# Two head groups of a dilated-attention trunk in Strassen block form

## The chip, the cores and the metric

The kernel runs on one core of one Trainium2 chip. The metric is the time of one execution on the device, in microseconds (us). The core has five instruction queues that run side by side and are tied together by semaphores: TensorE (PE, matrix products; PEld is its weight load), VectorE (DVE), ScalarE (ACT), GpSimd (POOL) and SyncE (SP). SP only issues transfers here; POOL issues the transfers that add to their destination, and computes a little.

## The reference

A decoder trunk of two layers on a sequence of 512 tokens with 1024 channels, all float32. Layer 1 mixes tokens by attention: three groups of eight heads, each with its own window and dilation. Layer 2 mixes by causal pooling. A SwiGLU feed-forward block follows each. The part that the change touches is the attention:

```python
qkv = (h @ w_qkv).reshape(B, S, 3, 3, 8, 128)     # h: rmsnorm(x), 512 x 1024
for g, (window, dil) in enumerate(((128, 1), (512, 4), (2048, 16))):
    o, lse = dilated_window_attention(q_g, k_g, v_g, window, dil, slopes[g])
o = sum_g softmax_g(lse) * o_g
x = x + o.reshape(B, S, 1024) @ w_out
```

For each of the 8 heads there are thus 3 groups, and for each group one product for q, one for k and one for v, each 512 x 1024 by 1024 x 128.

## The kernel before

**Precision.** Each float32 operand is split into a high part and a low part (the rest). A product is three matmuls on each 128-wide slice of the contraction: high times high, high times low, low times high. A weight tile of 128 x 1024 is loaded into a buffer `raw`; `split` makes its high part on ScalarE (L92) and its low part on VectorE (L93, raw minus high). In the "lean" form the low part is made otherwise: ScalarE writes the high part (L146) and its negative (L147), and POOL issues a transfer that adds the weight from memory onto that (L149).

**Plain and block form.** A plain product (`Product`, lines L329, L330, L332) of a group's q or k is 8 slices x 3 = 24 matmuls with 512 columns. The block form (`seven`, whose matmuls are L461 to L463 in `mult`) computes q and k of one group together as a 2 x 2 block matrix product by a Strassen scheme: 7 products of half-size blocks instead of 8, each 4 slices x 3 = 12 matmuls of 256 columns, 84 in all. Its weights (`Pair`) come as corners: two tiles of 128 x 1024 and a half tile by SP (L170 to L172), and one adding transfer by POOL (L173). They are split as "b", "s", "m" and "l"; "m" needs two additions on VectorE first (L189, L190). The other operand is the normalized input in block sums, `T`, made by `prepare(k)` for k = 0 to 3: L578, L582, L583, L587 and eight splits. Copies and additions (L489, L502, L510, L515, L516) put the seven products together.

**Order of head 0 and head 1.** Head 0 is plain in all groups. Head 1's three groups (`NSOLO = 3`) are plain too; from then on each group is in block form. The values of head 0 and 1 are plain, later ones in block form (`values12`, L632 to L634). Between products stand the attention steps: `scores0` (L716 to L725), `scores12` (L736 to L750), `merge` (L769 to L786, which scales the probabilities of both kinds: L783 on VectorE, L786 on ScalarE), `turn0` and `turn12` (transposes L799 and L820 on TensorE, copies L803, L805, L821, and L806, L825 on VectorE), and `output` (L837, L838, L844). They are hung into `seven` and `values12` as hooks by `between`.

**What sets the order.** The program's code gives an order of calls, and a scheduler of the framework lays the instructions of each engine out in a fixed sequence. Weights are pulled in by `pump`: a load when a buffer of `raw` (4) is free, a split when a buffer of `w` (5) or `half` (2) is free.

**The last head.** With head 7 the input x is loaded a second time (`xN`, L983, eight transfers of 128 x 512 by POOL) into the buffers that part of `T` occupied, for the residual sum. The output projection's weights are three plain tiles, two block pairs (`w_outp`), one plain tile. `summed` (L1022 to L1024) makes the block sums for it.

Of the kernel before, what the change touches and what calls it, by code (L numbers as in the profile page):

```python
# [15 lines left out]
P = 128  # L16
S = 512
# [22 lines left out]
NPLAIN = 4  # L40
WARM = 5
NOUT = 3
NSOLO = 3
PARTS = ((0, 2, False), (2, 10, True), (10, 18, True), (18, 22, False))
ENDS = 5
BACK = {"blocks": 3, "sums": 7}
# [19 lines left out]
def trunk(ctx: ExitStack, tc: tile.TileContext, xT, xN, norms, w_first, w_qk, w_qkp, w_v0, w_v0p, w_v12, w_out, w_outp, w_pair, w_down, w_dblock, w_pin, w_pgrp,  # L66
# [173 lines left out]
    for h in range(HEADS):  # L240
        if h == 0:
            plain(*[w_qk[u] for u in range(len(QK) - NF)])
        for g in range(3):
            if h == 1 and g < NSOLO:
                plain(*[w_qk[len(QK) - NF + 2 * g + c] for c in range(2)])
            elif h:
                pairs(w_qkp[3 * h - 3 - NSOLO + g])
        if h == 0:
            plain(w_v0[0], w_v0[1])
        elif h % 2 == 0:  # L250
            pairs(w_v0p[h // 2 - 1])
        else:
            pairs(w_v12[h // 2, 0], w_v12[h // 2, 1], shift=APART)
    plain(*[w_out[m] for m in range(NOUT)])
    pairs(w_outp[0])
    pairs(w_outp[1])
    plain(w_out[NOUT])

    def ffn_plan(layer):
# [340 lines left out]
    with tc.tile_pool(name="opool", bufs=1) as opool:  # L600
        early = [opool.tile([P, 2, S], F32R, tag=f"o{k}", name="early") for k in range(K2)]
        with tc.tile_pool(name="apool", bufs=1) as apool:
# [158 lines left out]
            def merge(h):  # L761
# [22 lines left out]
                for r in range(NT):  # L784
                    v = s12[:, r]
                    nc.scalar.activation(v, v, AF.Copy, scale=co[:, 1, r:r + 1])  # L786

            T0 = []

            def turn0(h):  # L790

                s0 = A[h]["s0"]
                if not T0:
                    T0.append(apool.tile([P, 2 * NT - 1, P], F32, name="t0"))
                    nc.vector.memset(T0[0], 0.0)
                own, before = T0[0][:, :NT], T0[0][:, NT:]
                p = ps()
                for b in range(NT):
                    nc.tensor.transpose(blk(p, b), s0[:, b, :P], ident)  # L799
                pb = p.rearrange("p (b q) -> p b q", b=NT)  # L800
                for j in range(NT):
                    c = slice(j * NI, (j + 1) * NI)
                    nc.scalar.copy(before[c, :, :c.stop], pb[c, 1:, :c.stop])  # L803
                    if j < NT - 1:
                        nc.scalar.copy(own[c, :, c.stop:], pb[c, :, c.stop:])  # L805
                    nc.vector.transpose(own[c, :, c], s0[c, :, P:])  # L806
                A[h]["t0"] = own, before
# [3 lines left out]
            def turn12(h):  # L811

                s12 = A[h]["s12"]
                if not T12:
                    T12.append(apool.tile([P, 2, NT, P], F32, name="t12"))
                    nc.vector.memset(T12[0][:, 1], 0.0)
                t12 = T12[0]
                p = ps()
                for r in range(NT):
                    nc.tensor.transpose(blk(p, r), s12[:, r, :P], ident)  # L820
                nc.scalar.copy(t12[:, 0].rearrange("p r k -> p (r k)"), p)  # L821

                for j in range(NT):
                    c = slice(j * NI, (j + 1) * NI)
                    nc.vector.transpose(t12[c, 1, :, c], s12[c, :, P:])  # L825
                A[h]["t12"] = t12
# [28 lines left out]
                 + [(late12[:, 0], late12[:, 1]), tuple(late)])  # L855
            H, T, o = {}, {}, []

            def prepare(k):

                h, t = normed(0, k, rows["row"], Held("raw"), Held("raw"))  # L860
                for i in range(2):
                    held["h", k + i * K2], b = slot("h")
                    H[k + i * K2] = b[:, 0], b[:, 1]
                    split(*H[k + i * K2], h.t[:, i * S:(i + 1) * S])
                T["11", k] = halves_of(*H[k])[0]
                T["21", k], T["22", k] = halves_of(*H[k + K2])
                for i, names in enumerate((("1", "2"), ("3", "4"))):
                    if k < 2:
                        held["t", k, i], b = slot("t")
                        b = b[:, 0], b[:, 1]  # L870
                    else:
                        c = k - 2 + 2 * i
                        b = x_tile(c, "tx", F32R), x_tile(c + K2, "tx", F32R)
                    split(*b, t.t[:, i * S:(i + 1) * S])
                    for name, v in zip(names, halves_of(*b)):
                        T[name, k] = v
                h.done()
                t.done()

            OP2 = {}  # L880
# [75 lines left out]
            for c in range(2):  # L956
# [1 line left out]
                if c == 0:  # L958
                    scores0(0)
                scaled_by(VT[c], p, True)  # L960
                prepare(2 + c)
            scores12(0)
            turn_values(0)
            scatter(0)
            for h in range(1, HEADS):
                for g in range(3):
                    if h == 1 and g < NSOLO:
# [9 lines left out]
                if h == 1:  # L977
                    O = [opool.tile([P, 2, S], F32, tag=f"o{k}", name="o") for k in range(K2)]
                    o.extend(O[h % K2][:, h // K2] for h in range(HEADS))
                if h == HEADS - 1:  # L980
                    X[:] = [x_tile(k) for k in range(KC)]
                    for k in range(KC):
                        nc.gpsimd.dma_start(X[k], xN[:, k, :])  # L983
                if h % 2 == 0:
                    VT[:] = [apool.tile([P, S], F32, tag=tag, name="vt") for tag in ("row", "o0")]
                    seven(T, *VT, scratch, {3: [later(scores12, h)], 6: [later(scatter, h)]}, True)
# [7 lines left out]
                                                   + [later(halve, 4), later(halve, 5)]})  # L994
            for key in [key for key in held if key[0] in "ht"]:
                give(key)

            last = HEADS - 1

# [521 lines left out]
```

## Time and profile before

| what | us |
|---|---|
| median of 3 runs | 1187.49 |
| lowest and highest | 1187.47, 1188.08 |
| the profiled execution | 1187.43 |
| its span in the profile | 1185.5 |
| TensorE busy | 1176.8 |
| VectorE busy | 986.4 |
| ScalarE busy | 719.1 |

A row of the timeline has the start and the duration in us, the engine, the line, the operation, output and inputs by tile names, shapes, and how many such instructions follow each other. What stands in brackets is how long the engine was idle before and which instruction ended the idle time. A duration overlaps the next instruction, so the spacing of two instructions is read from their starts. The list of waits names an engine, line and tile, then whom it waited for: us in total, times, longest. A row of the transfers has the queue, how many, their size, and the median time from issue to landing.

### The profile page before, as it was taken

How to read it: one execution, taken by the hardware profiler on the slowest of the kernel's cores; microseconds unless marked ns; L12 is line 12 of the kernel's file. 1: busy time of each engine (PE TensorE's matmuls, PEld its weight loads, DVE VectorE, ACT ScalarE, POOL GpSimd, SP SyncE). 2: the span in 40 equal slices, each digit the busy share in tenths (PEclk: the TensorE clock that was granted, in tenths of full speed). 3: DMA queues.
4: the chain of work that ended last, by engine and by line, in shares of the span. 5: the costliest groups of instructions: out<-in, count | busy, mean ns of one | idle time of the engine just before them, and what ended most of it. 6: DMA issues, size and time to landing. Idle time of an engine off the chain costs nothing.

```text
span 1185.5 us, 25087 instructions
## 1 busy us (share of the span) xinstructions
PE 1176.8 (99%) x10006; PEld 1119.5 (94%) x10006; DVE 986.4 (83%) x1729; ACT 719.1 (61%) x1257; POOL 175.0 (15%) x172
## 2 busy tenths in 40 slices
PE   9999999999999999999999999999999999999997
PEld 7889999999999989889999999988889999999997
DVE  7978898889789889699988997656879998898875
ACT  6445564455456557747756775775575776676553
POOL 1111211111111112311111111122130111111100
PEclk9999999999999999999999999999999999999999
DMA  8346666666766557957777777798595777777732
GB/s 298 114 101 162 155 155 161 171 160 151 191 141 166 148 159 195 248 109 196 195 191 191 192 196 203 191 268 208 123 198 110 193 193 190 205 194 190 197 95 72
DMA packets 82837, 206.77 MB, mean 174 GB/s; under 512 B 7824, under 2 KB 13088, under 8 KB 82720
## 3 DMA queue, kind: packets, MB, share of 16 engines
q1 hardware_dynamic: 51376, 142.48, 36.7%
q0 software_dynamic: 31056, 62.41, 31.5%
q8 instruction: 78, 1.28, 0.4%
q14 instruction: 39, 0.32, 0.1%
q10 hardware_dynamic: 288, 0.29, 0.1%
HBM read 203.05 MB, written 2.10 MB: 173 GB/s over the span
## 4 chain that ended last, share of the span: by engine, by line
PE 98%; issue 1%; DMA 0%; DVE 0%; ACT 0%; POOL 0%; DVEq 0%; POOLq 0%; SPq 0%; ACTq 0%
PE ps L461 20%; PE ps L462 20%; PE ps L463 20%; PE ps L329 8%; PE ps L332 8%; PE ps L330 8%; PE ps L632 2%; PE ps L633 2%; PE ps L634 2%; PE ps L922 2%; PE ps L844 1%; PE ps L716 1%; PE ps L838 1%; PE ps L736 1%; PE ps L837 0%
## 5 line engine op out<-in xcount | busy, mean ns | idle before, releaser
L92 ACT ACTIVATE w<-raw 128x1024 fp32r<-128x1024 f32 x267 | 282.7, 1063 | 180.0 <-PE ps L463 71.9
L93 DVE TENSOR_TENSOR w<-raw,w 128x1024 fp32r<-128x1024 f32 x267 | 325.3, 1222 | 50.7 <-ACT w L92 46.8
L463 PE MATMUL ps<-far,w 128*128 128x256 f32 x896 | 246.9, 276 | 0.0
L461 PE MATMUL ps<-far,w 128*128 128x256 f32 x896 | 246.9, 276 | 0.0
L462 PE MATMUL ps<-far,w 128*128 128x256 f32 x896 | 246.9, 276 | 0.0
L461 PE MATMUL ps<-near,w 128*128 128x256 f32 x660 | 186.2, 282 | 0.0
L462 PE MATMUL ps<-near,w 128*128 128x256 f32 x660 | 182.8, 277 | 0.0
L463 PE MATMUL ps<-near,w 128*128 128x256 f32 x660 | 182.7, 277 | 0.0
L461 PEld LDWEIGHTS ps<-far,w 128*128 128x128 f32 x896 | 168.3, 188 | 0.1
L462 PEld LDWEIGHTS ps<-far,w 128*128 128x128 f32 x896 | 168.3, 188 | 0.1
L463 PEld LDWEIGHTS ps<-far,w 128*128 128x128 f32 x896 | 168.3, 188 | 0.0
L461 PEld LDWEIGHTS ps<-near,w 128*128 128x128 f32 x660 | 124.2, 188 | 0.4
L462 PEld LDWEIGHTS ps<-near,w 128*128 128x128 f32 x660 | 124.2, 188 | 0.0
L463 PEld LDWEIGHTS ps<-near,w 128*128 128x128 f32 x660 | 124.1, 188 | 0.0
L329 PE MATMUL ps<-near,w 128*128 128x512 f32 (+1 forms) x316 | 119.5, 379 | 0.0
L332 PE MATMUL ps<-near,w 128*128 128x512 f32 (+1 forms) x316 | 118.9, 376 | 0.0
L330 PE MATMUL ps<-near,w 128*128 128x512 f32 (+1 forms) x316 | 118.8, 376 | 0.0
L173 POOL DMA_DIRECT2D raw<-w_pair x36 | 43.6, 1210 | 298.6 <-DMA raw<-w_pair 119.4
L329 PEld LDWEIGHTS ps<-near,w 128*128 128x128 f32 x316 | 59.3, 188 | 10.9 <-ACT near L92 0.4
L330 PEld LDWEIGHTS ps<-near,w 128*128 128x128 f32 x316 | 59.5, 188 | 10.7 <-DVE near L93 0.2
L332 PEld LDWEIGHTS ps<-near,w 128*128 128x128 f32 x316 | 59.3, 188 | 10.8
L92 ACT ACTIVATE half<-rawhalf 128x512 fp32r<-128x512 f32 x83 | 52.2, 630 | 13.9 <-PE ps L463 11.8
(335 smaller groups left out, 2817.1 us busy)
## 6 DMA issues: line engine op xcount, KB each, us to landing
raw<-w_pair SPq DMA_DIRECT2D x80, 512.0 KB, 5.0
raw<-w_qkp SPq DMA_DIRECT2D x36, 512.0 KB, 4.2
raw<-w_pair POOLq DMA_DIRECT2D x36, 512.0 KB, 7.5
raw<-w_dblock SPq DMA_DIRECT2D x32, 512.0 KB, 4.5
raw<-w_v SPq DMA_DIRECT2D x18, 512.0 KB, 4.5
raw<-w_qkp POOLq DMA_DIRECT2D x18, 512.0 KB, 7.4
rawhalf<-w_pair SPq DMA_DIRECT2D x36, 256.0 KB, 5.1
raw<-w_dblock POOLq DMA_DIRECT2D x16, 512.0 KB, 7.3
```

Of the source, the lines that this page charges most:

```text
L92: nc.scalar.activation(hi, v, AF.Copy)
L93: nc.vector.tensor_tensor(lo, v, hi.bitcast(F32), op=OP.subtract)
L173: nc.gpsimd.dma_start(self.b.rearrange("p (a c) -> p a c", a=2), self.src[:, None, 3 * n:].to_broadcast([P, 2, n]), accum_op=OP.add)
L329: nc.tensor.matmul(self.p[:, cols], w[0][:, s], mh[:, cols], start=self.done == 0, stop=False)
L330: nc.tensor.matmul(self.p[:, cols], w[0][:, s], ml[:, cols], start=False, stop=False)
L332: nc.tensor.matmul(self.p[:, cols], w[1][:, s], mh[:, cols], start=False, stop=self.done == self.n)
L461: nc.tensor.matmul(dst, w.t[0][:, c], th, start=k == 0 and not on, stop=False, skip_group_check=on)
L462: nc.tensor.matmul(dst, w.t[0][:, c], tl, start=False, stop=False, skip_group_check=on)
L463: nc.tensor.matmul(dst, w.t[1][:, c], th, start=False, stop=k == n - 1, skip_group_check=on)
L632: nc.tensor.matmul(o, mh, wh, start=k == 0, stop=False)
L633: nc.tensor.matmul(o, mh, wl, start=False, stop=False)
L634: nc.tensor.matmul(o, ml, wh, start=False, stop=k == K2 - 1)
```

## The change

`NSOLO` goes from 3 to 1: head 1's first group stays plain, its second and third are done by `seven`. The weights of the first group are made in the lean form. `prepare(2)` and `prepare(3)`, which must now be done before head 1's second group and not only before its values, no longer stand between the two value products of head 0 but behind its scores and value turns. `prepare` no longer borrows two `raw` buffers: it has a tile `room` and one of the `temp` slots. The zeroing of the two turn tiles goes from VectorE (a memset) to ScalarE (a copy scaled by 0). The two block pairs of the output projection get `back=True`, which lets a step of theirs be held for some calls of `pump`. The eight `xN` loads are issued by SP, after the loop over heads.

```diff
-NSOLO = 3
+NSOLO = 1
...
             if h == 1 and g < NSOLO:
-                plain(*[w_qk[len(QK) - NF + 2 * g + c] for c in range(2)])
+                plain(*[w_qk[len(QK) - NF + 2 * g + c] for c in range(2)], lean=True)
             elif h:
                 pairs(w_qkp[3 * h - 3 - NSOLO + g])
...
-    pairs(w_outp[0])
-    pairs(w_outp[1])
+    pairs(w_outp[0], back=True)
+    pairs(w_outp[1], back=True)
...
+            def zero(t, n):
+                nc.scalar.activation(t, ones.to_broadcast([P, n]), AF.Copy, scale=0.0)
...
-                    nc.vector.memset(T0[0], 0.0)
+                    zero(T0[0].rearrange("p b k -> p (b k)"), (2 * NT - 1) * P)
...
-                    nc.vector.memset(T12[0][:, 1], 0.0)
+                    zero(T12[0][:, 1].rearrange("p r k -> p (r k)"), S)
...
+            class Room:
+                def __init__(self):
+                    self.t = apool.tile([P, 2 * S], F32, name="room")
+
             def prepare(k):
 
-                h, t = normed(0, k, rows["row"], Held("raw"), Held("raw"))
+                h, t = normed(0, k, rows["row"], Room(), Temp())
...
-                h.done()
                 t.done()
...
                 scaled_by(VT[c], p, True)
-                prepare(2 + c)
             scores12(0)
             turn_values(0)
             scatter(0)
+            prepare(2)
+            prepare(3)
...
-                if h == HEADS - 1:
-                    X[:] = [x_tile(k) for k in range(KC)]
-                    for k in range(KC):
-                        nc.gpsimd.dma_start(X[k], xN[:, k, :])
...
             for key in [key for key in held if key[0] in "ht"]:
                 give(key)
+            X[:] = [x_tile(k) for k in range(KC)]
+            for k in range(KC):
+                nc.sync.dma_start(X[k], xN[:, k, :])
```

The change moves instructions in three places that matter below. Line numbers of the changed kernel are up to six higher than the old ones from L788 on (L802 is the old L799, L823 the old L820, L1002 the new place of the old L983).

First, TensorE in head 1, about the two transposes of the probabilities (the tiles `s`) and the first scores of head 1 (`qk`). Before:

```order
L330 MATMUL ps<-early,w 128x512
L332 MATMUL ps<-early,w 128x512
L799 MATMUL ps<-ident,s_496 128x128 x4
L820 MATMUL ps<-ident,s_620 128x128 x4
L716 MATMUL ps<-qk_731,qk_701 32x32
L716 MATMUL ps<-qk_731,qk_701 32x64
```

After, about the first of them:

```order
L462 MATMUL ps<-near,w 128x256
L463 MATMUL ps<-near,w 128x256
L802 MATMUL ps<-ident,s_497 128x128 x4
L461 MATMUL ps<-near,w 128x256
L462 MATMUL ps<-near,w 128x256
L463 MATMUL ps<-near,w 128x256
```

Four plain products stood ahead of all the transposes and scores. Now 96 block matmuls stand ahead of the first transposes, 36 between these and the second, 12 between those and the scores, and 24 behind.

Second, VectorE from head 0's merge to the scaling L783, whose result the first transposes read. Before:

```order
L775 TENSOR_TENSOR mx<-st 128x8
L190 TENSOR_TENSOR raw<-raw 128x512
L776 TENSOR_TENSOR ex<-st,mx 128x16
L778 TENSOR_TENSOR dd<-ex,st 128x16
L779 TENSOR_TENSOR mx<-dd 128x8
L780 RECIPROCAL mx<-mx 128x8
L781 TENSOR_TENSOR co<-ex,mx 128x8
L783 TENSOR_SCALAR s_496<-s_496,co 128x160 x4
```

After:

```order
L93 TENSOR_TENSOR half<-rawhalf,half 128x512
L776 TENSOR_TENSOR ex<-st,mx 128x16
L93 TENSOR_TENSOR w<-raw,w 128x1024
L778 TENSOR_TENSOR dd<-ex,st 128x16
L93 TENSOR_TENSOR w<-raw,w 128x1024
L779 TENSOR_TENSOR mx<-dd 128x8
L502 TENSOR_TENSOR qk_762<-ps,first 128x512
L780 RECIPROCAL mx<-mx 128x8
L510 TENSOR_TENSOR sums<-ps,qk_762 128x512
L781 TENSOR_TENSOR co<-ex,mx 128x8
L189 TENSOR_TENSOR raw<-raw 128x512
L783 TENSOR_SCALAR s_497<-s_497,co 128x160 x4
```

Between the steps of the merge now stand a half tile and two weight tiles of the block form (L93), the putting together of the second group (L502, L510) and an addition for the next weights (L189).

Third, POOL's queue at the end of the heads, where the adding transfers of the output projection's weights are issued. Before:

```order
L173 DMA raw<-w_v 128x2x512 x2
L173 DMA raw<-w_outp 128x2x512
L983 DMA x<-xN 128x512 x4
L173 DMA raw<-w_outp 128x2x512
L983 DMA x<-xN 128x512 x4
```

On SP's queue after:

```order
L170 DMA raw<-w_outp 128x1024
L171 DMA raw<-w_outp 128x1024
L1002 DMA x<-xN 128x512 x8
L140 DMA raw<-w_out 128x1024
L172 DMA rawhalf<-w_pair 128x512 x2
```

POOL's two adding transfers of `w_outp` now follow each other; the eight loads of x stand on SP behind the last corner tile and ahead of the last plain tile. At the same place VectorE's row L677 (the last value quarter of head 7) moves ahead of the split of the second of two weight tiles; it stood behind both.

## The prediction

> **What bounds the kernel now.** First the page's busy times and its chain of waits, then TensorE's own list of waits.
>
> ```profile
> span 1185.5 us, 25087 instructions
> PE 1176.8 (99%) x10006; PEld 1119.5 (94%) x10006; DVE 986.4 (83%) x1729; ACT 719.1 (61%) x1257; POOL 175.0 (15%) x172
> ...
> PE 98%; issue 1%; DMA 0%; DVE 0%; ACT 0%; POOL 0%; DVEq 0%; POOLq 0%; SPq 0%; ACTq 0%
> PE ps L838 <- ACT t L805: 1.3, 1, 1.3
> ```
>
> The chain is TensorE for 98%. Between its first and last matmul TensorE waits long enough to be listed once: 1.3 us at L838, in the last head's output. So time can be won by giving TensorE less to do, and by that one wait; anything else matters only where it makes TensorE wait anew. The profiled execution took 1187.43 us, 1.9 more than its span and 0.06 below the median of 1187.49; I subtract from 1187.43.
>
> **Part 1: two groups in block form.** The timeline of TensorE, head 1 (before), then the same pieces in head 2, which already has the block form in the order that the changed program uses here:
>
> ```profile
> 65.72 0.48 PE L329 MATMUL ps<-early,w 128*128 128x512 f32 x1
> 87.58 0.60 PE L799 MATMUL ps<-ident,s 128*128 128x128 f32 x4
> 89.84 0.39 PE L632 MATMUL ps<-w,near 128*128 128x256 f32 x1
> 93.69 0.46 PE L740 MATMUL ps<-qk,qk 128*32 128x32 f32 x32
> ...
> 172.05 0.60 PE L799 MATMUL ps<-ident,s 128*128 128x128 f32 x4
> 172.41 0.37 PE L461 MATMUL ps<-near,w 128*128 128x256 f32 x1
> 176.59 0.60 PE L820 MATMUL ps<-ident,s 128*128 128x128 f32 x4
> 176.94 0.37 PE L461 MATMUL ps<-near,w 128*128 128x256 f32 x1
> 178.49 1.36 PE L716 MATMUL ps<-qk,qk 128*32 128x32 f32 x88
> 179.79 0.39 PE L461 MATMUL ps<-near,w 128*128 128x256 f32 x1
> 192.16 0.28 PE L632 MATMUL ps<-w,near 128*128 128x256 f32 x1
> ```
>
> Before, four products of 24 matmuls with 512 columns run from 65.72 to 87.58: 96 in 21.86 us, 228 ns each; the transposes and scores end at 89.84, so the stretch takes 24.12 us. Afterwards it holds 2 x 84 = 168 matmuls of 256 columns, in pieces of 96, 36, 12 and 24, with transposes, transposes and scores between. Head 2's last piece is 108 in 12.37 us (179.79 to 192.16), 114.5 ns each. So: 96 x 0.1145 = 10.99; transposes 0.36 (172.05 to 172.41); the 36, 4.18; transposes 0.35; the 12, 1.55; scores 1.30; 24 x 0.1145 = 2.75. Sum 21.48, **2.64 us less**, if nothing is late. Half the columns take half the time, so the seventh-of-eight count comes through whole.
>
> The Trainium skill (TensorE: Matmul & The Clock Gate, "Back-to-back issue gap") speaks against it: it gives a sustained spacing of 131 ns at 512 columns and 81 at 128. Between these 256 would cost about 98 ns (my estimate from that page), and 168 x 98 against 96 x 131 would be 3.9 us more. Head 2's rows say otherwise, and they decide.
>
> **Part 2: is VectorE in time?** This is the price. Rows of its queue that give the spacing of each kind of instruction, and a place of TensorE:
>
> ```profile
> 31.91 1.42 DVE L578 SCALAR_TENSOR_TENSOR raw<-x,nrm,row 128x512 f32<-128x512 f32 x2 [1.99 <-ACT row L931]
> ...
> 46.79 0.42 DVE L583 TENSOR_TENSOR raw<-raw 128x256 f32<-128x256 f32 x1
> 47.13 0.69 DVE L93 TENSOR_TENSOR near<-raw,near 128x512 fp32r<-128x512 f32 x1
> ...
> 48.67 1.22 DVE L93 TENSOR_TENSOR w<-raw,w 128x1024 fp32r<-128x1024 f32 x1
> 49.80 0.69 DVE L93 TENSOR_TENSOR near<-raw,near 128x512 fp32r<-128x512 f32 x1
> 50.40 0.89 DVE L719 SCALAR_TENSOR_TENSOR s<-ps,b 128x480 f32<-128x480 f32 x2
> 51.20 0.68 DVE L610 TENSOR_TENSOR vt<-ps,row 128x512 f32<-128x512 f32 x1
> ...
> 53.75 1.09 PE L689 MATMUL ps<-ident,vt 128*128 128x128 f32 x8
> ...
> 76.11 1.01 DVE L783 TENSOR_SCALAR s<-s,co 128x160 f32<-128x160 f32 x4
> ...
> 90.41 1.24 DVE L806 STREAM_TRANSPOSE t<-s 32x128 f32<-32x128 f32 x4
> ```
>
> From start to start: 0.34 us for 256 elements (46.79 to 47.13), 1.13 for 1024 (48.67 to 49.80), 0.60 for 512 (49.80 to 50.40), 0.80 for a score evacuation or reduction (50.40 to 51.20). By their durations 0.71 for one L578, 1.01 for the four L783, 1.24 for four stream transposes; tiny ones I put at 0.1.
>
> I count the new queue from 31.91, when the row of norms lets the preparation begin. To the first block tile stand 4 of 0.71, 10 of 0.60 and 2 of 0.34: 9.5 us, so 41.4. From that tile to the end of the four L783 stand 7 of 1.13, 29 of 0.60, 4 of 0.71, 6 of 0.34, four score steps, 11 tiny ones and the L783: 35.5 us, so 76.9. Hand-overs from ScalarE come on top, above all where the tile "m" needs L190, then ScalarE, then VectorE; I put 0.4, an estimate: **77.3**. TensorE reaches the transposes that read L783's result after 96 matmuls, at 65.72 + 10.99 = 76.7. By the sum without hand-overs the wait is 0.2, by the one with them 0.6; with all spacings 1% shorter it is nothing. I take 0.6, between 0 and 0.7. Before, TensorE came here only at 87.58, 10.5 us after L783 was done: that cover is what the block form spends.
>
> Behind L783 the queue leads to L516, the last group's evacuation: 4 of 1.13, 8 of 0.60, 2 of 0.34, two score steps, eight transposes, a tiny one, 14.2 us, so 91.5. TensorE, if it starts the transposes at 77.3, needs 0.36 + 4.18 + 0.35 + 1.55 + 1.30 + 2.75 to the values, 3.85 from there to L740 (89.84 to 93.69) and 0.2 to its second half, which reads that result: 91.8. A wait of 0, or of 0.6 if hand-overs and a late tile cost 0.9; I take 0.2. Two earlier places hold. Of the 35.5 us, 23 lead to the low part of the last operand of the first block product, 64.4, and TensorE takes it at 66.8. The second value tile is there at 54.0, and its transposes are the second half of L689, 54.3. Head 1 in sum: 2.64 - 0.6 - 0.2 = **1.85 us won**, between 1.3 and 2.64.
>
> **Part 3: what costs nothing.** The first group's low parts: VectorE loses two splits (2.3 us, counted above), ScalarE gains two copies, POOL two issues behind the block tiles' own. Even if ScalarE made both (four passes of 1.06, the row of ScalarE below) only after the row at 31.9, and four POOL issues of 1.2 and the slowest landing below, 10.4, came on top, they would be there at 51.3; TensorE takes the first at 65.72 - 48 x 0.228 = 54.8. The zeroing of the two turn tiles leaves VectorE for ScalarE, which is 61% busy; without that cover VectorE's queue has two passes of 512 and 896 elements more, 1.6 us. Each block group brings three loads by SP and one adding transfer in place of two loads; the first group's stand in SP's queue where its plain tiles stood, some 30 us ahead of use, and the preparation no longer holds two raw buffers that they need.
>
> **Part 4: the wait at L838.** POOL, ScalarE and VectorE around it; then the transfers issued from 408 to 411 with their time to landing; last the landing times of all adding transfers of line L173:
>
> ```profile
> 410.08 1.20 POOL L173 DMA_DIRECT2D raw<-w_outp  x1 [26.84 <-DVE far L771]
> 412.12 2.24 POOL L983 DMA_DIRECT2D x<-xN  x4 [0.84 <-PE ps L633]
> 420.56 1.06 ACT L92 ACTIVATE w<-raw 128x1024 fp32r<-128x1024 f32 x1 [5.21 <-DMA raw<-w_outp]
> 422.79 0.68 DVE L677 TENSOR_TENSOR v<-ps,sums 128x512 f32<-128x512 f32 x1
> 431.09 0.25 ACT L805 COPY t<-ps 32x128 f32<-32x128 f32 x1
> raw<-w_outp SPq DMA_DIRECT2D x2, 512.0 KB, 5.7
> raw<-w_outp POOLq DMA_DIRECT2D x1, 512.0 KB, 10.4
> DMA to landing us min/median/max: 6.4/7.5/10.4
> ```
>
> ScalarE stood 5.21 us for the adding transfer of the first output block, which took 10.4 us where the median of all such is 7.5. VectorE then split that tile, did L677 and the rest up to L1024; ScalarE followed; the copies of L805 ended at 431.34, and TensorE waited. The change does two things here. L677 goes ahead of the split, which takes 0.60 off what follows it: the wait falls from 1.3 to 0.7. And xN goes by SP. If the adding transfer then landed in 7.5, 2.9 us sooner, the wait would be gone. But four of xN's loads are let go at the same moment as before, and two loads of 512 KB run beside. Between 0 and 1.3 I take 0.6, the swap alone. The remaining loads on SP stand behind xN until the last head's values end; the one output tile behind it is needed a stage later.
>
> **Sum.** 1187.43 - 1.85 - 0.6 = 1184.98; I forecast **1184.9 us**, 0.22% under the median. 0.2% (2.4 us) is about what a measurement can tell from no change.
>
> **Rivals.**
> - Everything is in time: VectorE's hand-overs cost nothing and the transfer lands in 7.5. 1187.43 - 2.64 - 1.3 = 1183.5. For it: 76.9 against 76.7, a few rows' rounding. Chance 0.20.
> - The gain is half given back: both waits of part 2 at their upper ends (1.3), and the transfer lands 0.6 later than now, so that the swap is eaten: 1187.43 - 2.64 + 1.3 = 1186.1. For it: VectorE's queue has no free place from 31.91 to 92, and xN on SP's queue meets it. The Trainium skill (DMA: Bandwidth & Descriptors, "Issuing engines are not separate DMA queues") says that all transfers run on the same 16 engines whoever issues them. By that rule moving xN clears nothing; the 10.4 us with two loads of SP beside it agree so far. Chance 0.26.
> - Slower: VectorE's in-order queue ahead of L783 stalls on a hand-over. Each microsecond past 76.7 is TensorE's. The gain is spent at 79.9, and 82.3 makes it 0.2% slower: three waits like the one at 31.91 (1.99 us) would give 83.3, and 1187.43 - 2.64 + 6.6 - 0.6 = 1190.8. Against it: the tiles in that stretch are loaded early. Chance 0.09.
> - Short pieces pay: all 168 matmuls spaced like the 12 between transposes and scores, 1.55 / 12 = 129 ns, are 21.7 us, with 2.0 of transposes and scores 23.7; 0.4 is won instead of 2.64, so 1187.43 - 0.4 + 0.8 - 0.6 = 1187.2. Head 2's 36 in 4.18 and 108 in 12.37 deny it. Chance 0.02. It is the direction of the skill's spacing above, which by my estimate would give 1191.3.
>
> **How the numbers follow.** The forecast has 0.43. Faster: 0.43 + 0.20 = 0.63; within 0.2%: 0.26 + 0.02 = 0.28; slower 0.09. The range goes from just under the first rival, 1183.4, to past the second, 1186.9, and leaves the slower ones out.
>
> **What would show it.** Part 1: 168 matmuls of L461 to L463 at 114 ns between L769 and the first L632, 21.5 us with no idle. Part 2: idle of some 0.6 us before the transposes after the first 96, released by L783, and little before L740. Part 3: no TensorE wait in the first group. Part 4: a wait at L838 of about 0.7, and ScalarE's 5.21 near what it was. I am wrong if L783 ends after 78, or if L838's wait grows.

## The result

| | before | after |
|---|---|---|
| median, us | 1187.63 (22 runs) | 1186.24 (22 runs) |
| lowest to highest | 1186.80 to 1189.90 | 1185.39 to 1187.48 |
| profiled execution | 1187.43 | 1186.38 |
| its span | 1185.5 | 1184.6 |
| start of TensorE's last row | 1178.59 | 1176.81 |

The ratio of after to before is 0.9986, with a 95% interval of 0.9980 to 0.9992: 1.4 us faster, where 1184.9 against 1187.49 was forecast, 2.6 us. The time lies in the range, and nearest to the rival in which half is given back (1186.1). The page of the changed kernel, and TensorE's list of waits:

```profile
span 1184.6 us, 25273 instructions
PE 1175.2 (99%) x10078; PEld 1121.2 (95%) x10078; DVE 989.8 (84%) x1737; ACT 725.2 (61%) x1267; POOL 174.7 (15%) x168
...
PE 94%; DVE 2%; DMA 2%; issue 1%; ACT 1%; POOL 0%; POOLq 0%; DVEq 0%; SPq 0%; ACTq 0%
PE ps L908 <- DVE idle L905: 1.2, 1, 1.2
PE ps L841 <- ACT t L808: 0.8, 1, 0.8
PE ps L689 <- DVE vt L610: 0.3, 1, 0.3
```

The wait at L908 (L902 before the change, also 1.2) lies ahead of TensorE's first matmul. The chain now has VectorE, ScalarE and transfers in it, and there is a wait that was not there before, at L689. Head 1 in TensorE's timeline:

```profile
54.63 0.55 PE L689 MATMUL ps<-ident,vt 128*128 128x128 f32 x3 [0.32 <-DVE vt L610]
66.06 0.33 PE L769 MATMUL ps<-far,const 128*128 128x64 f32 x2
66.20 0.36 PE L461 MATMUL ps<-near,w 128*128 128x256 f32 x1
...
77.48 0.28 PE L463 MATMUL ps<-near,w 128*128 128x256 f32 x1
77.80 0.66 PE L802 MATMUL ps<-ident,s 128*128 128x128 f32 x4
78.21 0.36 PE L461 MATMUL ps<-near,w 128*128 128x256 f32 x1
82.38 0.60 PE L823 MATMUL ps<-ident,s 128*128 128x128 f32 x4
84.33 1.36 PE L716 MATMUL ps<-qk,qk 128*32 128x32 f32 x88
88.48 0.28 PE L632 MATMUL ps<-w,near 128*128 128x256 f32 x1
92.25 0.57 PE L740 MATMUL ps<-qk,qk 128*32 128x32 f32 x32
92.75 0.39 PE L632 MATMUL ps<-w,near 128*128 128x256 f32 x1
```

Set beside the rows of before: TensorE comes to the stretch 0.48 us later (65.72 to 66.20), spends 22.28 us in it instead of 24.12, and is at the values' second half 1.33 us sooner (94.08 to 92.75). By the last head it gains another 0.46, so that its last row comes 1.78 us sooner. The span shrinks only by 0.9: the rest is lost behind TensorE. Three things are to be explained: the wait at L689, the 0.46, and the loss at the end.

### The profile page after: what moved, and what is told of

Read it like the earlier page. It is cut to its first block, busy times and chain, and to the rows that moved or that the text cites. A ratio compares the mean times of both kernels' runs of the same rounds, so it can differ in the third digit from the quotient of the medians.

```text
span 1184.6 us, 25273 instructions
## 1 busy us (share of the span) xinstructions
PE 1175.2 (99%) x10078; PEld 1121.2 (95%) x10078; DVE 989.8 (84%) x1737; ACT 725.2 (61%) x1267; POOL 174.7 (15%) x168
## 3 DMA queue, kind: packets, MB, share of 16 engines
q8 instruction: 79, 1.29, 0.4%
## 4 chain that ended last, share of the span: by engine, by line
PE 94%; DVE 2%; DMA 2%; issue 1%; ACT 1%; POOL 0%; POOLq 0%; DVEq 0%; SPq 0%; ACTq 0%
PE ps L461 21%; PE ps L462 21%; PE ps L463 21%; PE ps L329 6%; PE ps L330 6%; PE ps L332 6%; PE ps L928 2%; PE ps L632 2%; PE ps L634 2%; PE ps L633 2%; DMA raw<-w_outp 1%; PE ps L847 1%; PE ps L716 1%; PE ps L841 1%; PE ps L736 1%
## 5 line engine op out<-in xcount | busy, mean ns | idle before, releaser
L93 DVE TENSOR_TENSOR w<-raw,w 128x1024 fp32r<-128x1024 f32 x267 | 325.4, 1222 | 48.2 <-ACT w L92 44.3
L461 PE MATMUL ps<-near,w 128*128 128x256 f32 x692 | 195.1, 282 | 0.0
L462 PE MATMUL ps<-near,w 128*128 128x256 f32 x692 | 191.4, 277 | 0.0
L463 PE MATMUL ps<-near,w 128*128 128x256 f32 x692 | 191.4, 277 | 0.0
L461 PEld LDWEIGHTS ps<-near,w 128*128 128x128 f32 x692 | 130.1, 188 | 0.4
L462 PEld LDWEIGHTS ps<-near,w 128*128 128x128 f32 x692 | 130.2, 188 | 0.0
L463 PEld LDWEIGHTS ps<-near,w 128*128 128x128 f32 x692 | 130.0, 188 | 0.0
L329 PEld LDWEIGHTS ps<-near,w 128*128 128x128 f32 x316 | 59.3, 188 | 11.0 <-ACT near L92 0.4
L332 PEld LDWEIGHTS ps<-near,w 128*128 128x128 f32 x316 | 59.3, 188 | 10.9
L330 PEld LDWEIGHTS ps<-near,w 128*128 128x128 f32 x316 | 59.4, 188 | 10.6 <-DVE near L93 0.2
L92 ACT ACTIVATE half<-rawhalf 128x512 fp32r<-128x512 f32 x85 | 53.4, 630 | 14.8 <-PE ps L463 11.6
```

What stands on the lines that cost most here:

```text
L92: nc.scalar.activation(hi, v, AF.Copy)
L93: nc.vector.tensor_tensor(lo, v, hi.bitcast(F32), op=OP.subtract)
L329: nc.tensor.matmul(self.p[:, cols], w[0][:, s], mh[:, cols], start=self.done == 0, stop=False)
L330: nc.tensor.matmul(self.p[:, cols], w[0][:, s], ml[:, cols], start=False, stop=False)
L332: nc.tensor.matmul(self.p[:, cols], w[1][:, s], mh[:, cols], start=False, stop=self.done == self.n)
L461: nc.tensor.matmul(dst, w.t[0][:, c], th, start=k == 0 and not on, stop=False, skip_group_check=on)
```

## The experiments

Each kernel is the changed one but for the edit shown; its name stands in brackets. Their times mostly differ by less than the executions of one kernel do (some 2 us), so most verdicts rest on TensorE's times in the profile.

**Is it the block form? (solo3)**

```diff
-NSOLO = 1
+NSOLO = 3
```

> The changed kernel with head 1's second and third group back in plain form (all three groups, now with the lean low parts); everything else of the change stays. Theory (the block form carries the gain, the rest only the wait in the last head): the stretch from the first product behind L769 to the first L632 is 24.1 us again, against 22.3 in the changed kernel; the wait at L841 stays at 0.8. TensorE's end comes 1.3 to 1.9 us later than in the changed kernel, the time 0.0 to 0.7 under the kernel before, by the swap alone. Rival (the gain comes from what else was changed, for instance transfers that are no longer in the way): TensorE's end stays within 0.3 us of the changed kernel.

Measured: 1187.41 us, ratio to before 0.9995 (0.9985 to 1.0004). TensorE's last row starts at 1178.72, 1.91 after the changed kernel's. The stretch, in its timeline:

```profile
66.53 0.33 PE L769 MATMUL ps<-far,const 128*128 128x64 f32 x2
90.79 0.39 PE L632 MATMUL ps<-w,near 128*128 128x256 f32 x1
```

24.26 us from L769, against 22.42 in the changed kernel and 24.26 before the change (65.58 to 89.84). The block form alone is worth the 1.84 us. The rest of the change brings nothing in sum here: L769 comes 0.95 us later than before the change (66.53 against 65.58), with a wait of 0.6 at L689, and the shorter wait at L841 (0.5) wins about as much back. So the wait at L689 does not need the block form.

**The wait at L841: swap or xN?** First the swap is undone (noback).

```diff
-    pairs(w_outp[0], back=True)
-    pairs(w_outp[1], back=True)
+    pairs(w_outp[0])
+    pairs(w_outp[1])
```

> The changed kernel without back=True for the two block pairs of the output projection. The only effect on the order of instructions: VectorE's L677 stands behind the second of two weight splits again, as before the change. xN stays on SP. Theory (the swap made the wait at L841 shorter): the wait is 1.3 us again instead of 0.8, TensorE's end 0.5 later. Rival (xN's move to SP did it): the wait stays at 0.8, nothing moves.

Measured: 1186.50 us, 0.9991 (0.9981 to 1.0000); TensorE's last row at 1179.62. The wait is back, at 1.5 us, and in the profiled execution it does more than it takes. TensorE's timeline, then two stretches, of 10 and of 3.3 us (TensorE busy, then the granted clock, the transfers' share and GB/s); below them the changed kernel's 10 us:

```profile
430.78 0.49 PE L841 MATMUL ps<-t,v 128*128 128x128 f32 x2 [1.55 <-ACT t L808]
430.00:440.00 10.00, 9.21 (x47) 0.83 0.11 28
431.90:435.20 3.30, 3.30 (x17) 0.50 0.32 83
```

```profile
430.00:440.00 10.00, 9.99 (x59) 1.00 0.11 28
```

After a wait of 1.55 us the granted clock was 0.83 over these 10 us, and 0.50 in a part of them. Pairs of L840 and L841 that start 0.22 us apart in the changed kernel start 0.42 apart here, and between L841 and the next stage another 1.6 us were lost in this execution. The kernel before waited 1.3 at this place and kept its clock at 1.00.

This execution was the slowest of the ten of this kernel (1188.91 us; the others took 1185.94 to 1187.46), so the clock does not fall each time. The same mean clock of 0.997 over the whole execution is on record for four of the 81 executions of the kernel before that ran beside the experiments (1189.75 to 1190.22 us), and for none of the 106 of the kernels with the swap; that those four lost their clock at this wait is likely, but they have no trace. So the swap is confirmed. The wait itself is 0.3 to 1.1 us in the twelve traces with the swap and 1.3 and 1.5 in the two without; the 0.46 us is what it is worth in the two executions compared, and the distance from this edge comes on top. The Trainium skill (TensorE: Matmul & The Clock Gate, "What's actually happening") puts the fall to half the clock after an idle window of about 3.4 us. The trace agrees with the half (0.50 from 431.90 to 435.20), but here a wait of less than half of that window was followed by it.

Then xN is moved away from the adding transfer altogether, by an edge that queues it on POOL behind the second such transfer (xlast):

```diff
-            for k in range(KC):
-                nc.sync.dma_start(X[k], xN[:, k, :])
...
             halve(last)
+            with tc.issue_after(adds[-1]):
+                for k in range(KC):
+                    nc.gpsimd.dma_start(X[k], xN[:, k, :])
```

> The changed kernel with the eight xN loads on POOL behind both adding transfers of the output projection, so that none of them runs beside the first of these. Theory (the first adding transfer lands late because four of xN's loads share the transfer engines with it): it lands in about 7.5 us instead of 10.5, ScalarE stands some 3 us less than 5.3, the wait of 0.8 us at L841 is gone, TensorE's end 0.8 earlier. Rival (the loads of its own pair are what it shares with): it still takes over 9 us and the wait stays above 0.4.

Measured: 1185.32 us, 0.9979 (0.9969 to 0.9990). The landing times of the output projection's weights, and ScalarE's wait for them:

```profile
DMA to landing us min/median/max: 3.0/5.8/10.2
ACT w L92 <- DMA raw<-w_outp: 5.1, 1, 5.1
```

In the changed kernel these are 3.1/6.3/10.5 and 5.3. The theory falls: the adding transfer, issued at 408.9, takes 10.2 us although the first load of xN is issued only at 418.1, and the wait at L841 stays at 0.6. What runs beside it are the two loads of the second pair; that these make it slow was not tried. Which queue xN takes, and when, is nothing to this wait. For the queue this agrees with the Trainium skill (DMA: Bandwidth & Descriptors, "Issuing engines are not separate DMA queues"), by which all queues share one set of engines. And yet the median is 0.9 below the changed kernel's, with TensorE's end only 0.16 sooner. That pointed behind TensorE.

**The loss at the end.** The changed kernel once more (again), and beside it one with xN on POOL at its old place (poolx):

> The changed kernel, unaltered, beside the two below on one chip. Theory (the wait at L689 comes from the landing of the first loads and is different in each execution; the rest of TensorE's times is fixed): L769 again between 65.8 and 66.6, the stretch from there to the first L632 22.4 us within 0.05, 1186.0 to 1186.6 in the median. Rival (the times of head 1 are as fixed as the others): L769 at 66.06 as before.

```diff
+                if h == HEADS - 1:
+                    X[:] = [x_tile(k) for k in range(KC)]
+                    for k in range(KC):
+                        nc.gpsimd.dma_start(X[k], xN[:, k, :])
...
-            X[:] = [x_tile(k) for k in range(KC)]
-            for k in range(KC):
-                nc.sync.dma_start(X[k], xN[:, k, :])
```

> The changed kernel with xN back on POOL at its old place; the swap at L677 stays, and SP's queue is eight transfers shorter. With xN moved behind both adding transfers TensorE's end came 0.16 us earlier in the profile, but the median was 0.9 under the changed kernel's: something behind TensorE's end, or chance. Theory (eight more transfers on SP cost the tail: one issue of the last outputs took 1.35 us there against 0.33 before the change): 0.4 to 0.9 us under the changed kernel in the same job, wait at L841 0.8 as in the changed kernel. Rival (the tail differs by chance between executions): within 0.3 us of the changed kernel.

Measured on one chip: 1186.23 us unaltered (0.9987, 0.9978 to 0.9996; L769 at 66.61, as late as the theory allowed), 1185.68 with xN on POOL (0.9986, 0.9977 to 0.9995; the wait at L841 was 0.3). The medians are 0.55 apart, in ranges that overlap, and the two ratios to the kernel before are nearly the same: the times do not settle it. What settles it is the tail, from the start of TensorE's last row to the end of the span, over all profiled executions:

| xN's queue | kernels | tail, us |
|---|---|---|
| POOL | before, xlast, best2, best3, poolx | 6.91, 6.85, 6.80, 6.94, 7.08 |
| SP | after, again, noback, vtfirst, nolean, shift36, shift48 | 7.79, 7.85, 7.48, 7.69, 7.80, 7.59, 7.72 |
| SP, plain form | solo3 | 7.28 |

No value of the second row reaches down to the first (shift0, with xN on POOL, has 6.9 too). SP issues the last outputs there: eight tiles `x`, and behind them three tiles `ends`. Its issues of before, after, and of poolx (for the eight the least, middle and longest ns; for the three start and duration in us):

```profile
L1368 SPq DMA_DIRECT2D out<-x x8: 332/333/424, 1174.4 to 1179.4; - x8
1180.33 1.30 SPq L1434 DMA_DIRECT2D out<-ends  x3
```

```profile
L1374 SPq DMA_DIRECT2D out<-x x8: 332/372/1355, 1172.6 to 1178.4; - x8
1178.90 1.74 SPq L1440 DMA_DIRECT2D out<-ends  x3
```

```profile
L1375 SPq DMA_DIRECT2D out<-x x8: 332/372/1127, 1171.9 to 1177.5; - x8
1177.96 1.42 SPq L1441 DMA_DIRECT2D out<-ends  x3
```

One issue took 1.36 us in the changed kernel against at most 0.42 before. Counted from the start of TensorE's last row, the three last issues end after 3.04 us before, 3.83 in the changed kernel and 3.26 in poolx, and from there to the end of the span it is 3.9, 4.0 and 3.8: in the changed kernel nearly all of the loss lies in when SP has issued its last outputs. The 1.13 us of poolx are still covered, because the three start at 1.84 there and at 1.74 before, where SP stands idle ahead of them; behind the 1.36 us they start at 2.09 and take 0.4 longer. But this is not the whole cause either. In solo3 all issues are as short and as early as before, and the time from the last of them to the end of the span is 4.2 us; over all profiles it is 3.7 to 3.9 with xN on POOL and 3.95 to 4.4 with xN on SP. That xN on SP goes with a tail some 0.8 us longer is shown; by which mechanism is open.

**The wait at L689.** VectorE and ScalarE of the changed kernel, from the first hand-over to the value tile:

```profile
37.08 0.69 DVE L93 TENSOR_TENSOR near<-temp,near 128x512 fp32r<-128x512 f32 x1 [0.77 <-ACT near L92]
52.56 1.42 DVE L578 SCALAR_TENSOR_TENSOR room<-x,nrm,row 128x512 f32<-128x512 f32 x2
53.88 0.69 DVE L610 TENSOR_TENSOR vt<-ps,row 128x512 f32<-128x512 f32 x1
72.29 1.23 DVE L93 TENSOR_TENSOR w<-raw,w 128x1024 fp32r<-128x1024 f32 x1 [0.34 <-ACT w L92]
76.81 0.93 DVE L783 TENSOR_SCALAR s<-s,co 128x160 f32<-128x160 f32 x4
```

```profile
34.95 0.63 ACT L92 ACTIVATE half<-rawhalf 128x512 fp32r<-128x512 f32 x1 [1.04 <-DMA rawhalf<-w_qkp]
35.49 1.05 ACT L146 ACTIVATE w<-raw 128x1024 fp32r<-128x1024 f32 x1
36.44 0.61 ACT L92 ACTIVATE near<-temp 128x512 fp32r<-128x512 f32 x1
```

ScalarE stood 1.04 us for a half tile of the second block pair, then made a copy of the lean form (L146), and only then the high part that VectorE waited for, 0.77 us. From there VectorE's queue runs without a gap to 53.88, where the value tile is late. The list gives TensorE's wait there as 0.32, but it counts only what lies behind the modelled end of the matmul before; by the starts, the fifth transpose of L689 comes 0.60 us after the fourth (54.03 to 54.63) where the others stand 0.11 apart, so that 0.49 is lost. How long the hand-over is differs between executions, and the wait at L689 follows it, in eight executions whose order of instructions is the same up to here:

| | xlast | shift48 | shift36 | shift0 | after | poolx | again | noback |
|---|---|---|---|---|---|---|---|---|
| VectorE's idle at 37 us | 0.34 | 0.53 | 0.64 | 0.65 | 0.77 | 0.80 | 1.33 | 1.42 |
| TensorE's wait at L689 | none listed | none listed | 0.2 | 0.2 | 0.3 | 0.4 | 0.9 | 1.0 |

Each microsecond of hand-over above about 0.4 is TensorE's. What differs is the landing of that half tile: 5.4 us from its issue in xlast, 5.8 in the changed kernel, 6.4 in again and noback. From L769 on the times are fixed: 22.42 us to the first L632 in the changed kernel, 22.46 in its repetition. Now the two L578 are queued behind the value tile (vtfirst):

```diff
+            with tc.issue_after(last_vt):
+                prepare(2)
-            prepare(2)
             prepare(3)
```

> The changed kernel with the preparation of the third block pair queued on VectorE behind L610 for the second value tile; it stood ahead of it, with two passes L578. Theory (the wait at L689 is those two passes in front of the value tile, with a hand-over from ScalarE ahead of them that comes out differently in each execution): no wait at L689 in any case, TensorE begins the block form 0.3 to 0.5 us earlier than in the changed kernel, 65.6 to 65.8; L783 ends no earlier, so 0 to 0.4 of it is waited for again at L802. Time 0.2 to 0.5 us under the changed kernel. Rival (the value tile is late for another reason, the hand-over): a wait of 0.2 or more stays at L689.

Measured: 1186.73 us, 0.9994 (0.9984 to 1.0003). The waits of TensorE and the hand-over on VectorE:

```profile
PE ps L802 <- DVE s L783: 1.3, 1, 1.3
...
73.21 1.23 DVE L93 TENSOR_TENSOR w<-raw,w 128x1024 fp32r<-128x1024 f32 x1 [0.82 <-ACT w L92]
77.72 0.93 DVE L783 TENSOR_SCALAR s<-s,co 128x160 f32<-128x160 f32 x4
```

The wait at L689 is gone, L769 comes at 65.76, and TensorE waits 1.3 us at L802 instead of 0.2. I had allowed 0.4. The scheduler had put the split of a half tile into the place that came free; it was missing as a filler before the weight tile "m", where VectorE now idles 0.82 us instead of 0.34. What VectorE saved in one place it owed here in the next.

That edit and xlast's together (best2):

> Both: the third block pair's preparation behind the value tile, and xN on POOL behind both adding transfers. Theory (the two effects are in different places and add): 0.2 to 0.5 under the run with xN moved alone, 1184.8 to 1185.1. Rival (what VectorE saves early is waited for at L802): the same as with xN moved alone, 1185.3.

Measured: 1186.10 us, 0.9987 (0.9978 to 0.9996); the wait at L802 is 1.4. The rival was right: nothing is added, and it is no faster than xlast.

**How tight is VectorE's queue?** Two passes more on VectorE (nolean):

```diff
-                plain(*[w_qk[len(QK) - NF + 2 * g + c] for c in range(2)], lean=True)
+                plain(*[w_qk[len(QK) - NF + 2 * g + c] for c in range(2)])
```

> The changed kernel with the first group's two weight tiles split in the old way, low part on VectorE: two passes of 1.13 us more in VectorE's queue ahead of L783, two copies less on ScalarE, two adding transfers less. Theory (TensorE waits for VectorE's queue at L802, with no slack): L783 ends some 1.5 to 2.3 us later than in the changed kernel (77.7), and TensorE's wait there grows from 0.2 to between 1.5 and 2.5. Rival (the queue has slack, and the hand-overs from ScalarE that the copies delay decide): L783 ends within 0.5 us of 77.7.

Measured: 1187.23 us in one run. L783 ended at 78.5, 0.7 us later than in the changed kernel (77.7), and TensorE, which came 0.5 earlier, waited 1.3 at L802 (the list puts it down to ScalarE's L786 behind the same merge). Only one of the two passes came into the queue that the theory speaks of. The other stands ahead of it, in time in which VectorE had nothing to do:

```profile
28.69 1.23 DVE L93 TENSOR_TENSOR w<-raw,w 128x1024 fp32r<-128x1024 f32 x1 [0.53 <-ACT w L92]
31.91 1.41 DVE L578 SCALAR_TENSOR_TENSOR room<-x,nrm,row 128x512 f32<-128x512 f32 x2 [1.99 <-ACT row L937]
```

In the changed kernel VectorE stands idle 3.59 us ahead of that L578. So 1.13 us came in, the hand-overs of 0.77 at 37 us and of 0.34 at 72 are not there, and 0.5 of new short waits are, the longest of 0.41 for TensorE's products at L502: about the 0.7. Neither theory fits: the queue is full, but the edit put less into it than I counted, and took hand-overs out. The first of these goes with the order of the loads. The half tile that ScalarE waited for is issued here at 27.0, right behind the first pair's; in the changed kernel it stands behind another load of SP (L170, 28.76) and is issued at 29.14:

```profile
26.53 0.90 SPq L172 DMA_DIRECT2D rawhalf<-w_qkp  x2
```

```profile
25.55 0.63 SPq L172 DMA_DIRECT2D rawhalf<-w_qkp  x1
28.76 0.33 SPq L170 DMA_DIRECT2D raw<-w_qkp  x1
29.14 0.43 SPq L172 DMA_DIRECT2D rawhalf<-w_qkp  x1
```

One addition less ahead of L783, with xN as in xlast (best3):

```diff
+            with tc.issue_after(merged[0]) if len(merged) == 3 else nullcontext():
+                nc.vector.tensor_add(a[:, :n], a[:, :n], b[:, :n])
+                nc.vector.tensor_add(a[:, n:], a[:, n:], a[:, :n])
-            nc.vector.tensor_add(a[:, :n], a[:, :n], b[:, :n])
-            nc.vector.tensor_add(a[:, n:], a[:, n:], a[:, :n])
```

> xN on POOL behind both adding transfers, and the addition L189 for the third group's weights behind L783 on VectorE; it stood ahead of it. Theory (VectorE's queue is what TensorE waits for at L802): L783 ends 0.6 us earlier against L769, no wait at L802, TensorE's stretch from L769 to the first L632 22.2 us instead of 22.4; the time 0.2 under the run with xN moved alone. Rival (the addition is missed later): a wait inside the third group's products of up to 1 us.

Measured: 1186.23 us, 0.9988 (0.9979 to 0.9996). The stretch, and a new wait (lines are two higher here: L771 is L769, L634 is L632, L742 is L740):

```profile
66.20 0.33 PE L771 MATMUL ps<-far,const 128*128 128x64 f32 x2
88.32 0.28 PE L634 MATMUL ps<-w,near 128*128 128x256 f32 x1
...
PE ps L742 <- ACT s L727: 0.2, 1, 0.2
```

22.12 us, with no wait at L802, as expected; then 0.2 is waited for at the scores behind it. 0.1 us is left, which no timing can tell. The median is no better than the unaltered kernel's on the same chip.

**The spacing of the matmuls.** The first 96 block matmuls of head 1 stand 117.8 ns apart (66.41, the second, to 77.48: 94 steps), not 114.5. In both kernels the 256-column matmuls have two spacings, 113.3 and 117.8; a row of products mostly keeps one until other work or other operands interrupt it. The addresses of the operands were the suspect, and three other places of the weights in their buffers were tried, with the order of instructions unchanged:

```diff
-    def pairs(*srcs, shift=LINE // 4, back=False):
+    def pairs(*srcs, shift=36, back=False):
```

> The changed kernel with the weights of the block form 36 elements into their buffers instead of 16; the order of all instructions is the same. In the changed kernel the 256-column matmuls of the attention come at two spacings, 113.3 and 117.8 ns, in runs that change only at interruptions; in the feed-forward parts, where the two operands' addresses stand 112 bytes apart within 256 (weights below), all are at 113.3. Theory (the spacing depends on where the two operands lie against each other): all of L461 to L463 in the heads and the output projection go to 113.3 ns, which takes 0.5 us off head 1, 1.8 off the later heads and 0.7 off the output projection, 3.0 us in all at most. Rival (the spacing depends on what interrupted the stream, not on addresses): no group changes its level and the time stays within 0.3 us. A second rival: the new distance is worse, more groups at 117.8 or above, and the time grows by up to 5 us.

Measured: 1194.93 us, 1.0055 (1.0040 to 1.0070). Then 48, and 0 (the latter with xN on POOL):

> The changed kernel with the weights of the block form 48 elements into their buffers instead of 16 (36 made the heads' matmuls 118 to 120 ns each). 48 elements are 192 bytes, a multiple of 64 like the 64 bytes of the changed kernel; 36 elements, 144 bytes, are not. Theory (what costs is a weight tile that doesn't begin at a multiple of 64 bytes): at least as good as the changed kernel, the heads' mean spacing 114.3 ns or less, TensorE's end within 0.5 us or up to 3 us earlier. Rival (the distance to the other operand decides, and 64 bytes are the best there is): worse by 1 us or more.

> The kernel with xN back on POOL at its old place, and the block form's weights at the start of their buffers (0 elements in, where the changed kernel has 16). The order of all instructions is that of the run with xN on POOL. 36 and 48 elements gave 155 and 132 of the heads' 201 products at about 118 ns, 16 gave 38. In the plain form the weights stand at 0 and 512 columns take 227 ns, twice 113.5. Theory (the place of the weights in memory against the other operand decides, and the plain form's place has no loss): the heads' products all near 113.3 ns, TensorE's end 2 to 3 us earlier than in the run with xN on POOL, 1182.7 to 1183.7. Rival (any place but 16 is worse): more products at 118, 2 to 6 us slower than that run.

Measured: 1191.13 us (one run) and 1196.20 us, 1.0070 (1.0056 to 1.0083). From the starts of all 256-column matmuls, averaged over each product's 12:

| weights at element | 16 (after) | 48 | 36 | 0 |
|---|---|---|---|---|
| mean spacing from 92 to 440 us, ns | 114.3 | 116.2 | 117.8 | 118.1 |
| of these 201 products, at about 118 or above | 38 | 132 | 155 | 155 |
| TensorE's last row, us | 1176.81 | 1181.68 | 1185.71 | 1187.51 |
| time, us | 1186.24 | 1191.13 | 1194.93 | 1196.20 |

The last piece of head 2, 108 matmuls, in the changed kernel and with the weights at element 0:

```profile
178.46 0.38 PE L461 MATMUL ps<-near,w 128*128 128x256 f32 x1
190.83 0.28 PE L632 MATMUL ps<-w,near 128*128 128x256 f32 x1
```

```profile
181.73 0.39 PE L461 MATMUL ps<-near,w 128*128 128x256 f32 x1
194.79 0.28 PE L632 MATMUL ps<-w,near 128*128 128x256 f32 x1
```

12.37 us against 13.06, that is 114.5 and 120.9 ns each. Of the 201 products 54 are value products (L632 to L634), whose weights the edit does not move. Of the 147 whose weights it moves, 30 are at about 118 at 16 elements, 125 at 48, and all at 36 and at 0. All three theories were wrong and the suspect right: where the weights lie decides some 10 us, and 16 elements is the best of the four. The rivals that expected a loss had it too small: at most 5 and 6 us, where 8.7 (36) and 10.5 (0, against poolx) were lost. It is not the weights' own place alone: in the feed-forward parts nearly all weights stand at element 0, beside other operands, and nearly all matmuls are at 113 to 114 ns, in the changed kernel and in shift0 alike. At 16 both spacings occur, also in the same product of the seven in different groups, so the place is not all; what sets the choice at an interruption is open. My guess in the run with 48, that multiples of 64 bytes are all alike, is refuted.

## Why the prediction was right, and where it was off

**Part 1, the 2.64 us.** Right in its mechanism, and short in its size. The pieces measure 11.6 (with the wait), 0.41, 4.17, 1.95 for transposes and the 12, 1.29 and 2.86, sum 22.28. Without the wait of 0.2 that is 0.6 more than the 21.48. 0.32 us of it is the spacing of the first 96: 117.8 where I took 114.5 from a piece of head 2 that had the lower spacing nearly throughout. The short-pieces rival (129 ns) did not occur.

**Part 2, L783.** Forecast to end at 77.3 with a wait of 0.6; it ended near 77.7, with a wait of 0.2 (77.48 to 77.80, less one spacing), because TensorE was late too. The counted work holds: 44.7 us where I had 45.0. The 0.4 us for hand-overs measured 0.77 and 0.34 in this execution, the second at the tile "m" as said. At L740 nothing is waited for where I took 0.2. From the stretch's start to the values' second half, 1.81 us were won (28.36 to 26.55); with those two waits subtracted I had 1.85. That the two agree so well is luck: the matmuls took 0.6 us longer than I had summed, and the waits were 0.6 shorter (0.2 for 0.8), the shorter one because TensorE itself was late.

**The step that failed** is the sentence "Two earlier places hold". The second value tile was not there at 54.0 but at 54.57 (53.88 and 0.69), and TensorE lost 0.49 there and came to the stretch 0.48 late. (The first of the two places held.) I had subtracted no hand-over on the way to this place, though I did on the way to L783, and a margin of 0.3 us does not hold against one that ranges from 0.34 to 1.42.

**Part 3 and xN on SP.** TensorE never waited for a lean low part or for the zeroing. But the lean parts were not free: with them the half tile above is issued 2 us later, and L146 stands between it and the high part that VectorE waits for; in nolean there is no such hand-over and no wait at L689. (The two zeroing passes that I put at 1.6 us on VectorE took 0.48 and 0.81 in the kernel before; no sum uses them.) For the eight xN transfers on SP I looked at what stands behind them in the queue and at the transfers beside them. A tail longer by 0.8 us, which goes with them, was in no term: this is the other half of the missing gain.

**Part 4.** The wait went from 1.3 to 0.8 by the swap alone (0.46 us; 0.6 forecast), xN's queue did nothing to it, and the adding transfer took 10.5 us: as said, though the wait alone differs by as much as the 0.46 between executions. The clock behind a wait of 1.5 us was not foreseen.

In sum: 2.45 us forecast, 1.78 at TensorE's end (0.48 lost at L689, 0.14 less at L841), 0.9 by the span of the profiled execution, 1.4 by the medians. The rival that came nearest in time, half given back, had the wrong places: the two waits it raised stayed small.

Of all the runs xlast (0.9979) and poolx (0.9986) have the lowest medians, both with xN on POOL, 0.9 and 0.55 us under the changed kernel's. Both beat the kernel before. That they beat the changed one (0.9986, and 0.9987 when it was repeated) is not shown by the times, whose intervals overlap, and best3, which also has xN on POOL, has the same median as the repeated one.

## What to carry to other kernels

When a matrix product gets shorter, list every hand-over on the engine that feeds it, and test each margin against the largest one and not the mean: here a queue without gaps passed a delay on to whichever place had the least cover, and mending that place moved the wait to the next. Moving transfers to another queue went with a longer tail at the far end of that queue, so measure the tail from the last matmul to the end of the span as a term of its own. Take the spacing of a matmul from rows with the same operands at the same places in memory.

## What the runs showed of the hardware

- The same 256-column matmul takes 113.3, 117.8 or 120 ns from start to start, with all instructions in the same order, depending on where the weights lie in their buffers. Moving them by 16 elements (64 bytes) to the start of the buffer put TensorE's end about 11 us later (1176.12 to 1187.51, both with xN on POOL), over some 2,000 such matmuls.
- In one execution a wait of TensorE of 1.55 us was followed by a granted clock of 0.83 over 10 us (0.50 over 3.3 of them) and another 1.6 us lost; waits of 0.2 to 1.4 in the other traces were not.
- The first adding transfer of the output projection, 512 KB, took 9.8 to 10.8 us in all fourteen traces, with or without eight loads of 256 KB beside it.
- Eight transfers more on SP, some 760 us ahead of the end, went with a tail of 7.3 to 7.85 us instead of 6.8 to 7.1.
